# A two-layer hybrid attention block in fp32r on one core: compression tiles first in the head, a finer step of the compressed softmax, GpSimd work in smaller pieces, kept down chunks, and head banks from the ending layer's pool

## The chip, the cores and the metric

The kernel runs on one core of one Trainium2 chip. The time is device microseconds of one execution of the whole program, both layers, from the inputs in device memory to the output there. Weights are read from device memory in every execution. Lower is better.

## What is computed

For 512 tokens of width 1024 two layers are applied, each with a mixer and a feed-forward part:

```python
def hybrid_mixer(h, ...):
    q_nsa, kv_nsa, g_nsa, qkv_sb, g_merge = split(h @ w_in)
    q, k_cmp, k_slc, k_win = rope(...)          # v_cmp, v_slc, v_win as they are
    kc = gelu(blocks_of_32(k_cmp, stride 16) + pe @ w1 + b1) @ w2    # 31 compressed keys; vc alike
    o_nsa = g0 * softmax(q kc) vc + g1 * selected_attention(...) + g2 * window_attention(...)
    o_sb = stick_breaking_attention(...)        # 8 heads
    return (sigmoid(ga) * (o_nsa @ w_proj_nsa) + sigmoid(gb) * (o_sb @ w_proj_sb)) @ w_out
for l in range(2):
    x = x + rms_norm(hybrid_mixer(rms_norm(x)))
    h = rms_norm(x)
    x = x + rms_norm((gelu(conv3(h @ w_up)[gate]) * conv3(h @ w_up)[up]) @ w_down)
```

There are 8 query heads in 2 groups of 4, head width 64, and 2816 hidden units. With 8 selection blocks of 64 tokens and up to 16 selected, the selection takes all blocks, so that selected and window attention are both causal attention.

## The kernel before, in words

**Splits.** Every product is made of three matmuls in fp32r, hi x hi, lo x hi and hi x lo, where a value is the sum of a rounded part (hi) and the rest (lo). `h_hi` and `h_lo` hold the layer's input, normed, as [128, 8, 512]. Weights come through the class `Weights` (L54): a raw chunk of 128x1024 (512 KB) is fetched by SP's queue into one of three buffers, ScalarE (ACT) rounds it into `whi` (L105), and `wlo` is the difference (L106), made by VectorE (DVE), or by GpSimd (POOL) for 13 weights of a layer that are used beside the attention. `whi` and `wlo` have two buffers each. `gemm` and `mm` (L381 to L387) issue the matmuls; a `drain` runs one tile's to its end.

**Order of the work.** The kernel is written in Tile: the program says what reads and writes what, buffers and their counts say what may be in flight, and a scheduler fixes the order of each engine when the kernel is built, with `tc.high_priority()` as a hint. Instructions of an engine run in that fixed order, so one that waits holds up all that stand behind it. PSUM has a pool "pg" with six banks "bk" (closed before the attention), and helper banks with one buffer each, among them "f", which serves all the fill tiles of the attention: a fill tile can begin only when DVE has emptied the one before.

**Head of a layer.** The first six tiles of `w_m` in the order of `_cols` (L1284: the two key tiles kv(2) and kv(4), q tiles 0 and 1, then kv(0) and kv(1), the inputs of the compression) are computed in two halves of the tokens, the first half in `head_first` (L496) while the chain of the norm for the second half still runs, the second in `head_second` (L512). Each finished tile is handled by the loop at L667. `rope` (L610) copies the bank to `rf` on ACT, sends four `rs` transfers of 32 partitions through SP (L619), multiplies by cosine (`rt`) and sine (`rs`) and hands the two to a function that adds them: `k_tile` (L638) writes the split `kst` and sends two transfers, `q_tile` (L632) writes the split `qst`, `kc_done` (L662) writes `kd` and calls `spread` (L656), which sends `cstk` in four transfers. The second part of a rope is put off by one tile (`flush_later(1)`). The last tile, the compression's v, needs no rope.

Then come the value tiles `acc4` (L682), four banks of 128x280 with the values `vN` (hi on ACT at L704, lo on DVE at L706) and the gates' logits (L708, ACT); then `cst`, the split of `cstk` (L710 to L713), q tiles 2 and 3 (L715), and 32 compression matmuls into two more banks `cps` (L722). As there are six banks in all, the two of `cps` are those of the first two value tiles. The hidden layer of the compression follows (L735 to L746).

**Attention.** A pipeline over 32 subs, each one head of one block of 128 queries (`Sub`, loop at L978): scores `S`, maximum, exponential, scale of P by GpSimd (L924), transposes, and per pair of heads a product `pv`. `cmp_scores` (L846) is a generator with three stops that makes the softmax over the compressed keys for one group of heads (L854 to L870) and is stepped by the same loop, twice in each of two turns; `cmp_transpose` (L872) follows in the next turn:

```python
d = n - 15 * g_
if d == 2: cg = cmp_scores(g_)
if 2 <= d < 4:
    next(cg)
    next(cg, None)
if d == 4: pcs[g_] = cmp_transpose(g_)
```

Between the subs' matmuls the scheduler puts the fill tiles of the stick-breaking heads and of the merge: `sb_pair` (L772, emptied by `sbz` L781 and split at L786 to L789), `gate` (L795, emptied at L802), `sb_values` (L809). The stick-breaking attention, the output projections and the feed-forward part with its convolution follow.

**End of a layer.** The down projection has eight tiles of 22 row blocks in chunks of 8, 8 and 6. The last three (`TAIL_D`, m = 5, 6, 7) are computed for each half of the tokens apart (`down_tile`, L1250), so that the norm of the first half (`chain`, L426) runs beside the second half's; their weights are fetched and split twice. The pool with these banks is closed at the end of the layer, and the next head's six banks come from a new one, used in the order 1 to 5, 0.

Of the kernel before, what the change touches and what calls it, by code (L numbers as in the profile page):

```python
# [33 lines left out]
TAIL_D = 3  # L34

# [18 lines left out]
class Weights:  # L54
# [27 lines left out]
    def split(self, upto):  # L82
        while self.n_split <= min(len(self.items) - 1, upto):
# [4 lines left out]
            if fold:  # L88
# [8 lines left out]
                continue  # L97
            if dest is None:
# [5 lines left out]
            for c in ((slice(0, n),) if i else (slice(0, n // 2), slice(n // 2, n))):  # L104
                self.nc.scalar.copy(hi[:, c], raw[:, c])  # L105
                eng.tensor_sub(lo[:, c], raw[:, c], hi.bitcast(F)[:, c])  # L106
# [4 lines left out]
    def get(self):  # L111
        i = self.n_got
        self.n_got += 1
        self.ensure(i)
        return self.parts.pop(i)

# [42 lines left out]
def run_kernel(ctx, tc, xT, pos, inv, vec, pew, cw1, w_m, w_vn, w_pr, w_o, w_u, w_d, xmid, rot, out):  # L159
# [25 lines left out]
    for l in range(DEPTH):  # L185
# [19 lines left out]
        for i in dts:  # L205
            k0 = 0
            for n in DCH:
                it(w_d[l, i, :, k0 * 128:(k0 + n) * 128], n * 128)
# [315 lines left out]
    for l in range(DEPTH):  # L524
# [33 lines left out]
        pg = pg_ctx.enter_context(pool("pg", space=PSUM))  # L558
# [4 lines left out]

        banks = [bank() for _ in range(HEAD)]
        banks = banks[1:] + banks[:1]
# [15 lines left out]
        with temps(6) as ip:  # L581
# [85 lines left out]
            for i in head_second(banks, kept, n_pre=HEAD):  # L667
                b = banks[i]
                if i < 2:
                    k_tile(i, b)  # L670
                elif i < 4:
                    q_tile(i - 2, b)
                elif i == 4:
                    rope(b, kc_done)
                else:
# [3 lines left out]
                flush_later(1)  # L679

# [4 lines left out]
            for n_kt in (3, 3, 2):  # L685
# [11 lines left out]
                flush_later()  # L697
                kt += n_kt
# [10 lines left out]

            for v in range(2):  # L710
                src = cstk[:, v].rearrange("p (m s) -> p s m", s=8)
                nc.scalar.copy(cst[:, v, 0, :, :66], src)
                nc.vector.tensor_sub(cst[:, v, 1, :, :66], src, cst.bitcast(F)[:, v, 0, :, :66])  # L713
# [21 lines left out]
            for v in range(2):  # L735
                part = ip.tile([64, 132], F, name=nm("cpart"), tag="cpart")
                sums = ip.tile([64, 66], F, name=nm("csum"), tag="csum")
                nc.scalar.copy(part, cps[v][64:128, :132])
                nc.vector.tensor_add(part, cps[v][:64, :132], part)
# [99 lines left out]
        with temps(0) as nt, pool("pn", space=PSUM) as pn:  # L839
# [43 lines left out]
            class Sub:  # L883
# [35 lines left out]
                def scale(self):  # L919
# [4 lines left out]
                    nc.gpsimd.tensor_mul(pv, pv, st[:, None, 2:4, None].to_broadcast([128, self.i + 1, 2, 128]))  # L924
# [50 lines left out]
            pcs, cps_ = {}, {}  # L975
            subs[0].scores()
            at_sub = lambda n: subs[n] if 0 <= n < N else None
            for n in range(N + 3):  # L978
# [238 lines left out]
        with temps(5) as ft_:  # L1217
# [32 lines left out]
            def down_tile(m, tr, side=None):  # L1250
# [3 lines left out]
                for n_ in DCH:  # L1254
# [103 lines left out]
```

## Time and profile before

| | |
|---|---|
| time, median of 3 runs | 1655.97 us (1655.7 to 1656.61) |
| the profiled execution: its own time | 1653.88 us |
| its span, first to last instruction | 1652.2 us |
| mean granted TensorE clock in it | 0.989 of 2.4 GHz |
| busy: TensorE (PE), its weight loads (PEld) | 1609.0 us (97%), 1393.2 us (84%) |
| busy: DVE, ACT, POOL | 1118.2 (68%), 825.3 (50%), 211.1 us (13%) |
| DMA | 159.42 MB, mean 96 GB/s |

The table is one execution. A matmul of 512 columns starts every 0.23 us at full clock; the profile gives each a longer duration, since they are pipelined, so gaps between starts tell more than busy shares. The lines that matter stand in the section of rows below: where PE waited and for whom, the clock that was granted in a stretch, and the timelines of the engines that it waited for.

### The profile page before, as it was taken

To read this page: it belongs to the slowest core of one execution; us is meant where nothing else is said; L and a number is where in the kernel's file an instruction comes from. 1 tells how busy PE (TensorE), PEld (TensorE's weight loads), DVE (VectorE), ACT (ScalarE), POOL (GpSimd) and SP (SyncE) were. 2 spreads that over 40 slices of the span, in tenths; PEclk is the share of its full clock that TensorE was granted. 3 is DMA by queue.
4 is the path that set the end of the run, shared out by engine and by line. 5 is a ranking of instruction groups with operands and counts; after the bars stand their busy time and mean duration, and the time that the engine had idled before them with its cause. 6 is when DMAs were issued, how large, how long until landed. Compare 5 with 4: busy or idle time off the path is not lost.

```text
span 1652.2 us, 23212 instructions
## 1 busy us (share of the span) xinstructions
PE 1609.0 (97%) x8970; PEld 1393.2 (84%) x8970; DVE 1118.2 (68%) x1659; ACT 825.3 (50%) x1338; POOL 211.1 (13%) x252
## 2 busy tenths in 40 slices
PE   9899999999999999999999999999999999999997
PEld 9878887888998888888998788878889988888896
DVE  8775676767578777733677666677676687776235
ACT  6555565654555444423555455575536454444233
POOL 0034442120000000000000453322200000000000
PEclk9989999999999999999999999999999999999999
DMA  6521112114412233333664211112153132322344
GB/s 228 152 77 52 39 39 64 52 64 141 132 61 88 91 102 91 97 93 107 195 204 129 71 44 47 39 64 64 52 180 114 39 99 93 102 91 95 98 128 141
DMA packets 53501, 159.42 MB, mean 96 GB/s; under 512 B 6544, under 2 KB 12176, under 8 KB 53392
## 3 DMA queue, kind: packets, MB, share of 16 engines
q1 hardware_dynamic: 51088, 152.00, 29.0%
q0 software_dynamic: 1296, 4.72, 0.8%
q8 instruction: 70, 1.15, 0.3%
q10 hardware_dynamic: 1008, 1.23, 0.3%
q14 instruction: 39, 0.32, 0.1%
HBM read 144.30 MB, written 4.72 MB: 90 GB/s over the span
## 4 chain that ended last, share of the span: by engine, by line
PE 82%; DVE 8%; ACT 5%; issue 2%; DMA 2%; POOL 1%; SPq 1%; ACTq 0%; DVEq 0%; POOLq 0%
PE bk L382 56%; PE f L382 15%; PE pv L382 3%; PE Z L382 3%; PE S L382 2%; PE tp L935 2%; POOL sbt L1034 1%; DVE wlo L106 1%; DVE st L906 1%; DMA rs<-rf 1%; DMA x<-in_xT 1%; ACT whi L105 0%; ACT sbt L226 0%; ACT sbt L1058 0%; ACT sbw L226 0%
## 5 line engine op out<-in xcount | busy, mean ns | idle before, releaser
L105 ACT CAST whi<-wraw 128x1024 fp32r<-128x1024 f32 (+2 forms) x235 | 241.2, 1027 | 342.7 <-PE bk L382 254.3
L106 DVE TENSOR_TENSOR wlo<-wraw,whi 128x1024 fp32r<-128x1024 f32 (+2 forms) x209 | 248.8, 1191 | 184.1 <-ACT whi L105 181.4
L382 PE MATMUL bk<-h_hi,whi 128*128 128x512 f32 (+1 forms) x768 | 286.5, 374 | 2.1 <-ACT f_t L1260 1.7
L382 PE MATMUL bk<-h_hi,wlo 128*128 128x512 f32 (+1 forms) x768 | 286.4, 374 | 0.0
L382 PE MATMUL bk<-h_lo,whi 128*128 128x512 f32 (+1 forms) x768 | 286.2, 373 | 0.0
L382 PE MATMUL f<-h_hi,whi 128*128 128x512 f32 x448 | 184.4, 412 | 11.7 <-DVE gate L802 9.2
L382 PE MATMUL f<-h_lo,whi 128*128 128x512 f32 x448 | 179.1, 400 | 0.0
L382 PE MATMUL f<-h_hi,wlo 128*128 128x512 f32 x448 | 178.6, 399 | 0.0
L382 PEld LDWEIGHTS bk<-h_hi,whi 128*128 128x128 f32 x768 | 145.6, 190 | 27.7 <-ACT f_t L1260 1.9
L382 PEld LDWEIGHTS bk<-h_hi,wlo 128*128 128x128 f32 x768 | 145.5, 190 | 25.4 <-DVE wlo L106 0.4
L382 PEld LDWEIGHTS bk<-h_lo,whi 128*128 128x128 f32 x768 | 145.6, 190 | 24.8
L382 PE MATMUL bk<-ah,wlo 128*128 128x256 f32 (+1 forms) x484 | 161.7, 334 | 2.4 <-DVE wlo L106 2.4
L382 PE MATMUL bk<-ah,whi 128*128 128x256 f32 (+1 forms) x484 | 160.4, 331 | 0.0
L382 PE MATMUL bk<-al,whi 128*128 128x256 f32 (+1 forms) x484 | 160.2, 331 | 0.0
L382 PEld LDWEIGHTS f<-h_hi,whi 128*128 128x128 f32 x448 | 86.4, 193 | 30.6 <-DVE gate L802 10.0
L382 PEld LDWEIGHTS bk<-ah,wlo 128*128 128x128 f32 x484 | 91.8, 190 | 12.5 <-DVE wlo L106 3.4
L1228 DVE TENSOR_TENSOR cu<-bk,r 128x512 f32<-128x512 f32 x88 | 60.2, 687 | 61.2 <-PE bk L382 60.9
L382 PEld LDWEIGHTS f<-h_hi,wlo 128*128 128x128 f32 x448 | 85.9, 192 | 18.5
L382 PEld LDWEIGHTS f<-h_lo,whi 128*128 128x128 f32 x448 | 86.5, 193 | 15.5
L382 PEld LDWEIGHTS bk<-ah,whi 128*128 128x128 f32 x484 | 91.9, 190 | 8.7
L382 PEld LDWEIGHTS bk<-al,whi 128*128 128x128 f32 x484 | 91.9, 190 | 8.7
L382 PE MATMUL bk<-h_hi,wh 128*128 128x256 f32 x512 | 96.0, 285 | 0.0
(241 smaller groups left out, 3174.3 us busy)
## 6 DMA issues: line engine op xcount, KB each, us to landing
wraw<-in_w_u SPq DMA_DIRECT2D x88, 512.0 KB, 3.5
wraw<-in_w_m SPq DMA_DIRECT2D x72, 512.0 KB, 3.3
wraw<-in_w_d SPq DMA_DIRECT2D x44, 512.0 KB, 3.5
wraw<-in_w_d SPq DMA_DIRECT2D x22, 384.0 KB, 3.1
wraw<-in_w_pr SPq DMA_DIRECT2D x16, 512.0 KB, 3.6
wraw<-in_w_o SPq DMA_DIRECT2D x16, 512.0 KB, 3.5
rs<-rf SPq DMA_DIRECT2D x56, 64.0 KB, 2.8
wraw<-in_cw SPq DMA_DIRECT2D x4, 512.0 KB, 4.6
```

The costliest lines, as they stand in the source:

```text
L105: self.nc.scalar.copy(hi[:, c], raw[:, c])
L106: eng.tensor_sub(lo[:, c], raw[:, c], hi.bitcast(F)[:, c])
L382: last_mm[0] = nc.tensor.matmul(o, a, b, start=first, stop=last, skip_group_check=True)
L906: nc.vector.tensor_reduce(self.st[:, 0:2], self.S[:, :self.n].rearrange("p (j b k) -> p b j k", j=self.i + 1, b=2), axis=AX.XY, op=OP.max, ...
L935: nc.tensor.transpose(tp[:, b * 128:(b + 1) * 128], self.P[:, (c + b) * 128:(c + b + 1) * 128], ident)
L1034: nc.gpsimd.affine_select(out=d, in_=d, compare_op=OP.is_gt, fill=0.0, base=0, pattern=[[1, 128]], channel_multiplier=-1)
L1228: nc.vector.tensor_mul(u, b, r2)
```

## The change

There are five parts. (1) The tiles of the compression, k and v, come first in `_cols`, then the two key tiles and q tiles 0 and 1; the head loop follows, and the `cst` splits move into the loop of the value tiles, behind its first chunk. (2) The softmax of the compressed scores is stepped once per turn (turns 2 to 5), its transposes come in turn 6, the second group starts two turns earlier, and a `pv` product that needs it waits in a list until it is there. (3) GpSimd makes `wlo` in four pieces of 256 columns, and scales P in pieces of 256 columns. (4) The first two chunks of down tile 6 are split into the second token half of `h_hi` and `h_lo`, which is free then, and serve both halves, so that they are not fetched again. (5) The six banks of layer 1's head are taken from the pool of the ending layer, one by one as they come free and in their own order; that pool is closed behind the head, and a new one serves the value tiles, q tiles 2 and 3 and the compression.

```diff
@@ Weights.split @@
+            if isinstance(dest, tuple):
+                hi, lo = dest
+                raw = raw.rearrange("p (s c) -> p s c", c=256)
+                self.nc.scalar.copy(hi.whole(), raw)
+                eng.tensor_sub(lo.whole(), raw, hi.whole().bitcast(F))
...
-                eng.tensor_sub(lo[:, c], raw[:, c], hi.bitcast(F)[:, c])
+                step = (c.stop - c.start) // (4 if eng is self.nc.gpsimd else 1)
+                for c_ in range(c.start, c.stop, step):
+                    s = slice(c_, c_ + step)
+                    eng.tensor_sub(lo[:, s], raw[:, s], hi.bitcast(F)[:, s])
@@ class Strips @@
+    def whole(self):
+        return self.t()[:, self.k:self.k + 4, 256:]
...
@@ items @@
+                keep = i == KEPT and c < 2
+                if not (keep and j >= 8):
+                    it(w_d[l, i, :, k0 * 128:(k0 + n) * 128], n * 128,
+                       dest=(Strips(lambda: h_hi, 4 * c), Strips(lambda: h_lo, 4 * c)) if keep else None)
@@ banks of the head @@
-        banks = [bank() for _ in range(HEAD)]
-        banks = banks[1:] + banks[:1]
+        if l == 0:
+            pf_ctx = ExitStack()
+            pg = pf_ctx.enter_context(pool("pg", space=PSUM))
+            next_banks = [bank() for _ in range(HEAD)]
+        banks = next_banks
@@ head loop @@
-                if i < 2:
-                    k_tile(i, b)
-                elif i < 4:
-                    q_tile(i - 2, b)
-                elif i == 4:
+                if i == 0:
                     rope(b, kc_done)
+                elif i >= 4:
+                    q_tile(i - 4, b)
+                elif i >= 2:
+                    k_tile(i - 2, b)
                 else:
...
+            pf_ctx.close()
+            pg = pg_ctx.enter_context(pool("pg", space=PSUM))
@@ after the first chunk of the value tiles (before: behind them) @@
+                if kt == 0:
+                    for v in range(2):
+                        src = cstk[:, v].rearrange("p (m s) -> p s m", s=8)
+                        nc.scalar.copy(cst[:, v, 0, :, :66], src)
+                        nc.vector.tensor_sub(cst[:, v, 1, :, :66], src, cst.bitcast(F)[:, v, 0, :, :66])
@@ hidden layer of the compression @@
-                part = ip.tile([64, 132], F, name=nm("cpart"), tag="cpart")
+                part = ip.tile([64, 132], F, name=nm("cpart"), tag="cpart", bufs=2)
...
+                with tc.high_priority():
+                    nc.scalar.copy(part, cps[v][64:128, :132])
+                    nc.vector.tensor_add(part, cps[v][:64, :132], part)
@@ Sub.scale @@
-                    nc.gpsimd.tensor_mul(pv, pv, st[:, None, 2:4, None].to_broadcast([128, self.i + 1, 2, 128]))
+                    for j in range(self.i + 1):
+                        nc.gpsimd.tensor_mul(pv[:, j], pv[:, j], st[:, 2:4, None].to_broadcast([128, 2, 128]))
@@ loop over the subs @@
-                    d = n - 15 * g_
+                    d = n - 13 * g_
                     if d == 2:
                         cg = cmp_scores(g_)
-                    if 2 <= d < 4:
-                        next(cg)
+                    if 2 <= d < 6:
                         next(cg, None)
-                    if d == 4:
+                    if d == 6:
                         pcs[g_] = cmp_transpose(g_)
                 if s3 and s3.hm == 1:
-                    pv_pair(s3)
+                    pv_due.append(s3)
+                while pv_due and pv_due[0].g in pcs:
+                    pv_pair(pv_due.pop(0))
@@ down_tile @@
-                for n_ in DCH:
-                    drain(gemm(b[:, :w_], W.get(), *a_of(tr), range(k0, k0 + n_), first=k0 == 0,
+                for c, n_ in enumerate(DCH):
+                    keep = m == KEPT and c < 2
+                    wt = kept_d[c] if keep and tr is HALVES[1] else W.get()
+                    if keep:
+                        kept_d[c] = wt
+                    drain(gemm(b[:, :w_], wt, *a_of(tr), range(k0, k0 + n_), first=k0 == 0,
@@ end of a layer @@
             if last:
                 side_next.finish()
-        pf_ctx.close()
+                pf_ctx.close()
+            else:
+                next_banks = [bank() for _ in range(HEAD)]
@@ _cols @@
-    tiles = [kv(2), kv(4), q(0), q(1), kv(0), kv(1), q(2), q(3)]
+    tiles = [kv(0), kv(1), kv(2), kv(4), q(0), q(1), q(2), q(3)]
```

The change moves instructions on every engine. Three places, as the orders have them; lines of the changed kernel are some 30 to 40 higher.

Place 1, PE of layer 0, from the end of the last q tile (`bk_899` before, `bk_903` now) over the compression matmuls into two banks to a fill tile (`f`). Before (the first fill tile, `f_2182`, has 24 matmuls, of which the last three are shown):

```order
L382 MATMUL f_2182<-h_hi,whi_951 128x512
L382 MATMUL f_2182<-h_lo,whi_951 128x512
L382 MATMUL f_2182<-h_hi,wlo_952 128x512
L382 MATMUL bk_933<-cst_473,wh_63_722 128x132 x16
L382 MATMUL bk_934<-cst_473,wh_69_839 128x132 x16
L382 MATMUL f_2227<-h_hi,whi_2207 128x512
L382 MATMUL f_2227<-h_lo,whi_2207 128x512
```

Now:

```order
L413 MATMUL bk_903<-h_hi,whi_665 128x512
L413 MATMUL bk_903<-h_lo,whi_665 128x512
L413 MATMUL bk_903<-h_hi,wlo_666 128x512
L413 MATMUL bk_937<-cst_473,wh_60_712 128x132 x16
L413 MATMUL bk_938<-cst_473,wh_70_847 128x132 x16
L413 MATMUL f_2234<-h_hi,whi_955 128x512
L413 MATMUL f_2234<-h_lo,whi_955 128x512
L413 MATMUL f_2234<-h_hi,wlo_956 128x512
L413 MATMUL f_2234<-h_hi,whi_955 128x512
```

In before `bk_899` ends just ahead of `f_2182`, and the compression follows that fill tile; now it follows the q tile, and the first fill tile stands behind it.

Place 2, DVE of layer 0, the readers of the value banks (`vN`) and the ropes of q tiles 0 and 1 (`qst_4_104`, from `rt` and `rs`). Before:

```order
L706 SCALAR_TENSOR_TENSOR vN_732<-bk_733,rT_465,vN_732 128x2x64 x2
L630 TENSOR_TENSOR rt_593<-rt_593,rs_592 128x512
L706 SCALAR_TENSOR_TENSOR vN_732<-bk_734,rT_465,vN_732 128x2x64 x2
L706 SCALAR_TENSOR_TENSOR vN_732<-bk_735,rT_465,vN_732 128x2x64 x2
L706 SCALAR_TENSOR_TENSOR vN_732<-bk_736,rT_465,vN_732 128x2x64 x2
L623 TENSOR_TENSOR rs_639<-rs_639,cs_t_462 128x512
L620 TENSOR_TENSOR rt_685<-rf_683,cs_t_462 128x512
L636 SCALAR_TENSOR_TENSOR qst_4_104<-rt_593,qst_4_104 64x512 x2
L630 TENSOR_TENSOR rt_640<-rt_640,rs_639 128x512
L623 TENSOR_TENSOR rs_684<-rs_684,cs_t_462 128x512
L106 TENSOR_TENSOR wlo_952<-wraw_681,whi_951 128x1024
L664 TENSOR_TENSOR kd_477<-rt_685,rs_684 128x256x2
```

Now:

```order
L652 TENSOR_TENSOR rt_719<-rf_717,cs_t_462 128x512
L655 TENSOR_TENSOR rs_672<-rs_672,cs_t_462 128x512
L662 TENSOR_TENSOR rt_673<-rt_673,rs_672 128x512
L668 SCALAR_TENSOR_TENSOR qst_4_104<-rt_673,qst_4_104 64x512 x2
L655 TENSOR_TENSOR rs_718<-rs_718,cs_t_462 128x512
L662 TENSOR_TENSOR rt_719<-rt_719,rs_718 128x512
L668 SCALAR_TENSOR_TENSOR qst_4_104<-rt_719,qst_4_104 64x512 x2
L746 SCALAR_TENSOR_TENSOR vN_736<-bk_737,rT_465,vN_736 128x2x64 x2
L746 SCALAR_TENSOR_TENSOR vN_736<-bk_738,rT_465,vN_736 128x2x64 x2
L746 SCALAR_TENSOR_TENSOR vN_736<-bk_739,rT_465,vN_736 128x2x64 x2
L746 SCALAR_TENSOR_TENSOR vN_736<-bk_740,rT_465,vN_736 128x2x64 x2
```

The four `vN` pairs stood ahead of both `qst` (the second follows two rows below the ones shown) and now stand behind both; on ACT the gates of each value bank follow its `vN`, so they are moved too.

Place 3, DVE of layer 0, the end of the first softmax over the compressed keys (`cp`, `cm`) and the operation that empties the bank "f". Before:

```order
L860 TENSOR_TENSOR cp_1093<-cp_1093,cm_1096 128x512
L922 TENSOR_TENSOR st_1127<-st_1127,gates_111 128x2
L863 TENSOR_REDUCE cm_1096<-cp_1093 128x16
L864 RECIPROCAL cm_1096<-cm_1096 128x16
L867 TENSOR_TENSOR cm_1096<-cm_1096,gates_111 128x16
L802 TENSOR_TENSOR gate_2342<-f_2343,r_90 128x512
```

Now:

```order
L896 TENSOR_TENSOR cp_1097<-cp_1097,cm_1117 128x512
L958 TENSOR_TENSOR st_1126<-st_1126,gates_111 128x2
L899 TENSOR_REDUCE cm_1117<-cp_1097 128x16
L900 RECIPROCAL cm_1117<-cm_1117 128x16
L817 SCALAR_TENSOR_TENSOR sbz_2397<-f_2363,r_90 128x512
L903 TENSOR_TENSOR cm_1117<-cm_1117,gates_111 128x16
```

The operation that empties "f" (`gate_2342` before, `sbz_2397` now) stood behind the product of `cm` with the gates and now stands ahead of it.

## Rows read from the trace of the kernel before

**Rows 1.** The page: busy time, the chain's shares by engine, the DMA issues of the ropes.

```profile
PE 1609.0 (97%) x8970; PEld 1393.2 (84%) x8970; DVE 1118.2 (68%) x1659; ACT 825.3 (50%) x1338; POOL 211.1 (13%) x252
...
PE 82%; DVE 8%; ACT 5%; issue 2%; DMA 2%; POOL 1%; SPq 1%; ACTq 0%; DVEq 0%; POOLq 0%
...
rs<-rf SPq DMA_DIRECT2D x56, 64.0 KB, 2.8
```

**Rows 2.** Waits of PE by releaser: total us, times, longest.

```profile
PE f L382 <- DVE gate L802: 9.2, 4, 4.0
PE bk L382 <- DVE cst L713: 3.4, 2, 1.9
PE bk L382 <- DVE wlo L106: 2.4, 3, 1.4
...
PE bk L382 <- ACT f_t L1260: 1.7, 1, 1.7
```

**Rows 3.** Windows: length, busy us of each engine, granted clock, DMA share, GB/s.

```profile
76.00:88.00 12.00, 10.12 (x47) 9.05 (x46) 10.44 (x14) 6.11 (x9) 0.34 (x1) 0.72 0.46 134
99.00:126.00 27.00, 22.99 (x109) 18.58 (x109) 20.64 (x38) 11.38 (x32) 11.51 (x8) 0.87 0.22 70
190.00:260.00 70.00, 66.42 (x409) 55.54 (x408) 46.95 (x100) 37.16 (x95) 25.72 (x16) 1.00 0.11 39
814.00:832.00 18.00, 14.32 (x115) 13.69 (x113) 15.16 (x24) 12.62 (x21) 1.48 (x2) 1.00 0.76 249
```

**Rows 4.** Timeline of PE, compression of layer 0, and at 908: start us, us, instruction.

```profile
72.34 0.39 PE L382 MATMUL f<-h_hi,whi 128*128 128x512 f32 x1
...
77.55 0.39 PE L382 MATMUL f<-h_hi,wlo 128*128 128x512 f32 x1
79.82 1.43 PE L382 MATMUL bk<-cst,wh 128*128 128x132 f32 x10 [1.88 <-DVE cst L713]
...
85.75 0.73 PE L382 MATMUL f<-h_hi,whi 128*128 128x512 f32 x1
...
93.12 0.50 PE L382 MATMUL f<-h_hi,whi 128*128 128x512 f32 x1
...
908.27 0.50 PE L382 MATMUL f<-h_hi,whi 128*128 128x512 f32 x1
```

**Rows 5.** Timeline of SP's DMA issues, layer 0.

```profile
65.44 3.19 SPq L619 DMA_DIRECT2D rs<-rf  x4
...
73.44 2.42 SPq L660 DMA_DIRECT2D cstk<-kd  x4
```

**Rows 6.** Timeline of DVE, ropes and values of layer 0.

```profile
64.50 0.61 DVE L706 SCALAR_TENSOR_TENSOR vN<-bk,rT,vN 128x128 fp32r<-128x128 f32 x2
...
68.50 1.41 DVE L636 SCALAR_TENSOR_TENSOR qst<-rt,qst 64x512 fp32r<-64x512 f32 x2
...
70.55 0.69 DVE L623 TENSOR_TENSOR rs<-rs,cs_t 128x512 f32<-128x512 f32 x1
...
83.46 0.69 DVE L623 TENSOR_TENSOR rs<-rs,cs_t 128x512 f32<-128x512 f32 x1 [1.07 <-DMA rs<-rf]
```

**Rows 7.** Timeline of PE, first softmax of the compressed scores.

```profile
120.19 0.80 PE L382 MATMUL f<-h_hi,whi 128*128 128x512 f32 x1 [4.01 <-DVE gate L802]
```

**Rows 8.** Timeline of DVE, same place.

```profile
117.19 2.34 DVE L867 TENSOR_TENSOR cm<-cm,gates 128x16 f32<-128x16 f32 x1
119.45 0.68 DVE L802 TENSOR_TENSOR gate<-f,r 128x512 f32<-128x512 f32 x1
120.05 0.16 DVE L868 TENSOR_TENSOR cm<-cm,rowv 128x16 f32<-128x16 f32 x1
```

**Rows 9.** Timeline of GpSimd (POOL), ahead of and at the same place.

```profile
98.29 0.61 POOL L924 TENSOR_TENSOR P<-P,st 128x256 f32<-128x256 f32 x1 [1.83 <-ACT P L226]
...
117.16 2.34 POOL L106 TENSOR_TENSOR wlo<-wraw,whi 128x1024 fp32r<-128x1024 f32 x1 [0.40 <-ACT whi L105]
```

**Rows 10.** Timeline of PE, first head tile of layer 1.

```profile
828.29 0.39 PE L382 MATMUL bk<-h_hi,whi 128*128 128x256 f32 x1 [1.67 <-ACT f_t L1260]
```

More of the change, by code (lines that the diff above doesn't have):

```diff
@@ L34 @@
 TAIL_D = 3
+KEPT = 6
 ALL = slice(0, T)
@@ L97, in split @@
                 continue
+            if isinstance(dest, tuple):
[3 more added lines that the diff above has]
+                eng.tensor_sub(lo.whole(), raw, hi.whole().bitcast(F))
+                self.parts[i] = dest
+                self.n_split += 1
+                self.prefetch()
+                continue
             if dest is None:
@@ L115, in get, with __init__, __getitem__ @@
         return self.parts.pop(i)
+class Strips:
+    def __init__(self, t, k):
+        self.t = t
+        self.k = k
+    def whole(self):
+        return self.t()[:, self.k:self.k + 4, 256:]
+    def __getitem__(self, key):
+        c, e = key[1].start, key[1].stop
+        return self.t()[:, self.k + c // 256, 256 + c % 256:256 + c % 256 + e - c]
 class Fill:
@@ L204, in run_kernel @@
         dts = list(range(8 - TAIL_D)) + 2 * list(range(8 - TAIL_D, 8))
-        for i in dts:
+        for j, i in enumerate(dts):
             k0 = 0
-            for n in DCH:
-                it(w_d[l, i, :, k0 * 128:(k0 + n) * 128], n * 128)
+            for c, n in enumerate(DCH):
+                keep = i == KEPT and c < 2
+                if not (keep and j >= 8):
+                    it(w_d[l, i, :, k0 * 128:(k0 + n) * 128], n * 128,
+                       dest=(Strips(lambda: h_hi, 4 * c), Strips(lambda: h_lo, 4 * c)) if keep else None)
                 k0 += n
@@ L557, in run_kernel @@
         pg_ctx = ExitStack()
-        pg = pg_ctx.enter_context(pool("pg", space=PSUM))
         def bank():
             return pg.tile([128, T], F, name=nm("bk"), tag="bk", bufs=6)
-        banks = [bank() for _ in range(HEAD)]
-        banks = banks[1:] + banks[:1]
+        if l == 0:
[3 more added lines that the diff above has]
+        banks = next_banks
         with temps(0) as hp:
@@ L708, in run_kernel @@
                 nc.scalar.activation(gates[:, j], acc4[j][:, 256:280], AF.Copy, scale=rj)
[L710 to L713, printed above, removed]
             qst.append(slot("q1", "qst1", FR))
@@ L735, in run_kernel @@
             for v in range(2):
-                part = ip.tile([64, 132], F, name=nm("cpart"), tag="cpart")
+                part = ip.tile([64, 132], F, name=nm("cpart"), tag="cpart", bufs=2)
                 sums = ip.tile([64, 66], F, name=nm("csum"), tag="csum")
-                nc.scalar.copy(part, cps[v][64:128, :132])
-                nc.vector.tensor_add(part, cps[v][:64, :132], part)
+                with tc.high_priority():
+                    nc.scalar.copy(part, cps[v][64:128, :132])
+                    nc.vector.tensor_add(part, cps[v][:64, :132], part)
                 nc.vector.tensor_add(sums, part[:, :66], part[:, 66:])
@@ L975, in run_kernel @@
             pcs, cps_ = {}, {}
+            pv_due = []
             subs[0].scores()
@@ L1260, in down_tile @@
                 nc.scalar.activation(f_t[:, m, tr], b[:, :w_], AF.Copy, scale=g_post2[:, m:m + 1])
+            kept_d = {}
             last = l == DEPTH - 1
```

## Prediction

> **What bounds the kernel now.** I read the page first. TensorE (PE) is busy for 1609.0 us, 97% of the span, and the chain that ended last lies on PE for 82% [rows 1]. No part of the change removes a matmul that counts, so all it can win is PE's idle time and the stretches in which PE runs at the lower of its two clock levels. Next, the waits of PE grouped by what ended them [rows 2]: two long ones in the fill tiles "f" behind a VectorE (DVE) `gate` (4 waits, 9.2 us, the longest 4.0), two before the compression matmuls behind `cst` (3.4), three behind `wlo` of the down tiles (2.4), one behind `f_t` at the layer boundary (1.7). Each of the first two comes once per layer. Then the windows [rows 3]: around the compression matmuls (76 to 88 us) the granted clock is 0.72, around the softmax of the compressed scores (99 to 126) it is 0.87. A stretch whose mean is 0.72 holds 56% of its time at half speed: 0.56 x 12 = 6.7 us at 1.2 instead of 2.4 GHz, which costs 3.4 us; 0.87 over 27 us gives 7.0 us and 3.5. So each of these waits is paid twice: as idle time, and as a slow stretch right behind it. The `cst` wait costs about 1.9 + 3.4 = 5.3 us, the `gate` wait 4.0 + 3.5 = 7.5 us, per layer.
>
> **The change, part by part, in its order on PE.**
>
> *Compression tiles first.* In before PE reaches the end of the q tiles at 72.34, does one fill tile (24 matmuls, 72.34 to 77.55), waits until 79.82 for `cst`, does the 32 compression matmuls (until 85.75, slow), then the second fill tile, and begins the third at 93.12 [rows 4]. The change makes `cst` ready early (its cast now stands on ACT and DVE ahead of the last key tile's), but the scheduler drew two conclusions from it that cost something. The compression matmuls now come right behind the q tiles, with no fill tile ahead (place 1 of the order). And they write into the banks of the first two value tiles; these are free only when DVE and ACT have read them (`vN`, `gates`), and in the changed order these readers stand behind the ropes of both q tiles (place 2). The last of the six head tiles is now q1, whose rope needs a transfer through SP. SP issues four `rs` transfers in 3.19 us and four `cstk` in 2.42 [rows 5]; the rope of q1 now has eight `cstk` issues ahead of it instead of two. I reckon its last issue at about 71.3 (the fourth rope's four issues ended at 65.44 + 3.19 = 68.6 in before; six `cstk` more are 3.6 us, the tail of one `kst` pair less), its landing 2.8 us later [rows 1] at 74.1, then on DVE the product `rs` 0.69, a sum of the same size, `qst` 1.41, `vN` 0.61 [rows 6], and ACT's small `gates`: free at 77.5 to 78. PE arrives at 72.9 (the start of the head loses about 0.5: its first value tile waits for an ACT copy behind a weight cast). So a wait of about 5 us stands where one of 1.9 stood, followed by the slow stretch as before.
>
> That puts the first fill tile at about 77.9 + 5.9 = 83.8 instead of the second one at 85.75. Its end, about 90.2, is followed by a further wait: there is one bank for "f", it is emptied by DVE's `sbz`, and this now stands behind the ropes of q tiles 2 and 3 (in before the last of their `rs` was there at 83.46 [rows 6]; here the queue is later by the same 5 us, so about 88, and a product, two sums, the `cpart` sums and two `qst` pairs follow): about 93.2. So at 93.2 the change begins its second fill tile where before began its third: one fill tile behind. A tile is 24 matmuls in 77.55 + 0.23 - 72.34 = 5.4 us. **Loss 5.5 us in layer 0.** Fill tiles are not free work, they are all needed later, so this stays lost. In layer 1 the same order stands, and before begins its third fill tile at 908.27 [rows 4]; I reckon the second of the change at 907.2 by the same steps, one tile less 1.1: **loss 4.4**. Ends per layer: nothing, if SP runs ahead of my count so that only what `cst` cost before is left (or a gain of the 5.3 if even this goes), and 8, if the later `sbz` slips by one more rope.
>
> *Softmax one step per head, GpSimd in pieces.* In before a fill tile of PE waits 4.01 us, until 120.19 [rows 7]. The reason is on DVE: `gate`, which empties the one "f" bank, starts at 119.45, behind a 128x16 product (L867) that took 2.34 us, when its neighbour of the same size (L868) took 0.16 [rows 8]. GpSimd ran its `wlo` from 117.16 for 2.34 us [rows 9]: the two end together. With `wlo` in four pieces of 256 columns the block is bounded by one piece, which I take from the 128x256 scaling, 0.61 [rows 9]. The changed order also has the evacuation of "f" right behind the reciprocal and ahead of that product (place 3), so even that block no longer stands before it. The product started at 117.19, behind the reciprocal; an evacuation in its place takes 0.68, so PE resumes at 117.9 in the place of 120.19, and earlier by as much as DVE is ahead from not being blocked at the two earlier `wlo`s. That is 2.3 us of idle time; whether the slow stretch goes as well depends on what is left of the wait. Idle gaps of about 2 us were followed by half speed at 77.55 and not at the layer boundary (1.67) [rows 3, 4, 10], so what is left, 1.7 or less, is on the better side. Ends: 2.3 (clock still falls) and 7.5 (no wait at all). I take 5.4, near 2.3 + 3.5: **gain 5.4 per layer**.
>
> The Trainium skill ("SBUF — State Buffer", Who interferes with whom) says that a VectorE operation with two SBUF inputs and a GpSimd operation that reads SBUF exclude each other for a whole instruction, and that whichever starts first wins. The trace agrees with the first half (2.34 beside 2.34). By the second half the pieces also open gaps in which DVE can hold GpSimd up; that is the rival C below.
>
> *The other stalls of attention.* In 190 to 260 us PE is busy for 66.42 of 70 [rows 3]: some 3.6 us in gaps under 1.4 us. One step of softmax per head and smaller blocks take some of it away; the deferred output products and the scaling in pieces (0.61 for each 256 columns, more instructions on an engine that is busy 13%) put something new there. Bounds -2 and +3 per layer; I take **+1 per layer**, near the middle.
>
> *Kept down chunks, head banks.* Two weight chunks less per layer are 2 DMAs, 2 ACT casts, 2 DVE subtractions. PE doesn't get shorter; what counts is the wait behind `wlo` (2.4 in all) and the first head tile's wait for its bank behind `f_t` (1.7) [rows 2, 10]. With banks from the ending pool in turn the first head tile takes a bank that has long been free: gain 1.7. The `wlo` of the last tile's second chunk still stands behind the post chain on DVE, so I count little there: **2.0 in all**, ends 0 and 4. At the end of the kernel the same chunks may take **0.5** (0 to 1).
>
> **Sum**, against the profiled execution (1653.88): -5.5 + 5.4 - 4.4 + 5.4 + 2 x 1 + 2.0 + 0.5 = 5.4 us less, 1648.5. The median of the runs shown is 2.1 us above that execution, so about 1650.6: I say **1651**, 0.3% faster.
>
> **Rivals.** A change within 0.2% (3.3 us) is about what can't be told from none.
>
> A, slower. The new wait before the compression matmuls decides: it keeps its 5.5 and 4.4 (the order shows the readers behind the ropes), while at the softmax the clock still falls, so the gain there is 2.3 twice, and attention wins nothing: -9.9 + 4.6 + 2.5 = 2.8 worse; with 1 us lost per layer in attention, 5 worse: about 1661. It decides from the point at which the softmax gives less than about 3.7 a layer. For it: a residual wait of about 1.7 lies just under one that was followed by half speed. Chance 0.23.
>
> B, much faster. q1's transfers are issued in time, since SP waits less for DVE than I count, and the compression matmuls no longer wait. Then 5.3 and 7.5 per layer go, and the 2.5: 28 us, about 1628. Against it: SP's issues are a plain sum of durations of which none shrinks. Chance 0.07.
>
> C, no change. Terms cancel, within 3.3 us: about 1655. One way: GpSimd's pieces are held up by DVE operations of 0.69 each, 4 x 0.69 = 2.8 us more per `wlo`, and PE waits for that once per layer: 5.6 of the gain go. The rule of the page named above is that rival. Against it: GpSimd is idle most of the time between its `wlo`s. Chance 0.05 for this way, 0.20 for other cancelling.
>
> **How the numbers follow.** The forecast (3.3 to 15 us faster) has 0.45, B 0.07: faster 0.52; C, same 0.25; A, slower 0.23. The range reaches from 1641 (softmax waits gone wholly, 4 more, attention and boundary at their better ends, 6 more) to 1661 (A); B and the worst of A lie outside.
>
> **What would show it.** In the changed profile: the first compression matmul at 77 to 79 us, with a wait of 4 to 6 before it that ends with ACT `gates` or DVE `vN`, and a second fill tile that starts at about 93 and waits for `sbz`; no DVE operation of 128x16 over 0.9 us; the fill-tile wait near 116 under 2 us and the clock of that stretch 1.00; no wait for `f_t` at the boundary. The prediction is wrong if the compression matmuls start by 74, or if a wait of over 3 us stands in the fill tiles after 95 us.

## The result, and the profile after

The changed kernel takes 1667.76 us (median of 4 runs, 1667.15 to 1668.28) against 1655.84 of the kernel before: 1.0073 times, 95% interval 1.0055 to 1.0090. It is 12 us slower, outside the range that was forecast.

The page after, busy time of the engines, answers to [rows 1]:

```profile
PE 1605.1 (96%) x8970; PEld 1393.1 (84%) x8970; DVE 1097.0 (66%) x1655; ACT 820.5 (49%) x1334; POOL 239.1 (14%) x426
```

TensorE (PE) works as long as before; the span grew from 1652.2 to 1666.2 us. The time went into waits, so the waits of PE come first (total us, times, longest), against [rows 2]:

```profile
PE bk L413 <- ACT rf L648: 22.5, 3, 15.8
PE f L413 <- DVE sbz L817: 10.6, 3, 6.4
...
PE bk L413 <- ACT gates L748: 1.0, 1, 1.0
...
PE f L413 <- DVE gate L838: 0.9, 1, 0.9
```

The waits for `gate` fell from 9.2 to 0.9, and those for `cst` and `f_t` are gone. In their place stand 22.5 us in which a bank "bk" waits for ACT to copy a rope's tile out (`rf`), 15.8 of them in one piece, and 10.6 us for `sbz`. The windows (length, busy us of PE, PEld, DVE, ACT, POOL, granted clock, DMA share, GB/s), the first four those of [rows 3], the last one the place of the long wait:

```profile
76.00:88.00 12.00, 10.97 (x53) 9.36 (x52) 5.93 (x13) 6.96 (x15) 0.34 (x1) 0.76 0.25 77
99.00:126.00 27.00, 26.54 (x132) 21.82 (x133) 20.40 (x47) 18.48 (x48) 12.83 (x17) 0.93 0.26 79
190.00:260.00 70.00, 69.36 (x432) 58.69 (x430) 42.33 (x92) 39.72 (x97) 32.91 (x54) 1.00 0.14 54
814.00:832.00 18.00, 17.47 (x144) 17.14 (x143) 17.23 (x30) 11.91 (x23) 1.48 (x2) 1.00 0.60 194
866.00:890.00 24.00, 8.17 (x51) 7.96 (x51) 16.04 (x23) 8.11 (x12) 0.82 (x2) 0.64 0.61 169
```

The stages come some 7 us later than before, so a window doesn't hold quite the same work; still, three are better: PE is busy for 26.54 of 27 us around the compressed softmax (22.99 before), 69.36 of 70 in the attention (66.42), 17.47 of 18 at the layer boundary (14.32). With the windows moved by 7 us the three values are 27.00 at a clock of 1.00, 67.93 and 17.47, so the attention gained less than the row suggests. Two stretches are new and bad: from 866 to 890 PE is busy for 8.17 of 24 us, at a mean clock of 0.64, and from 84 to 104, just ahead of the softmax, for 13.58 of 20 at 0.71 (19.94 at 0.91 before).

By the start of the first matmul of each stage in PE's timeline, before and after: value tiles of layer 0 48.47 and 49.23, first down tile 700.58 and 707.98, value tiles of layer 1 864.42 and 883.70, last matmul 1641.47 and 1655.18. So layer 0 lost 7.4, the way from its down tiles to layer 1's value tiles 11.9 more, and the rest won 5.6 back.

The long wait in layer 1, in the timeline of PE (start us, us, instruction, idle time before it and what ended it):

```profile
867.59 0.28 PE L413 MATMUL bk<-h_hi,wh 128*128 128x256 f32 x1
883.70 0.83 PE L413 MATMUL bk<-wh,h_hi 128*128 128x280 f32 x2 [15.83 <-ACT rf L648]
```

And the timeline of ACT there:

```profile
865.61 1.06 ACT L648 COPY rf<-bk 128x512 f32<-128x512 f32 x2
...
872.69 0.58 ACT L648 COPY rf<-bk 128x512 f32<-128x512 f32 x1 [3.75 <-DMA rs<-rf]
876.50 1.14 ACT L736 CAST cst<-cstk 128x528 fp32r<-128x528 f32 x1 [3.22 <-DMA cstk<-kd]
880.13 1.26 ACT L682 CAST kst<-rt 64x512 fp32r<-64x512 f32 x2 [2.49 <-DVE rt L675]
881.41 0.59 ACT L648 COPY rf<-bk 128x512 f32<-128x512 f32 x1
882.02 1.14 ACT L736 CAST cst<-cstk 128x528 fp32r<-128x528 f32 x1
883.06 0.58 ACT L648 COPY rf<-bk 128x512 f32<-128x512 f32 x1
```

The first value tile starts at 883.70, right behind the last of the five ropes' copies (883.06 + 0.58), that of q1. The copies come late for two reasons, which the rows show. The third (872.69) waits for the `rs` transfers of an earlier rope, since each rope takes some of a few work buffers (a median of 2.3 us from issue to landing in this run, 2.8 in [rows 1]). The last two stand in ACT's fixed order behind the casts of `cst` and `kst`, which wait for `cstk` and for DVE's `rt`, and so for transfers too. In the built program the six head tiles of layer 1 stand in PSUM banks 7, 6, 5, 4, 3 and 2 in their order, and the value tiles in 2, 7, 6 and 5: the first one on the bank of q1.

In layer 0 the same kind of wait comes in smaller pieces, again in PE's timeline:

```profile
49.23 0.52 PE L413 MATMUL bk<-wh,h_hi 128*128 128x280 f32 x2 [2.82 <-ACT rf L648]
...
56.85 0.53 PE L413 MATMUL bk<-wh,h_hi 128*128 128x280 f32 x2 [3.86 <-ACT rf L648]
```

Then comes what was forecast for the compression, on PE and, below, on DVE:

```profile
79.53 4.75 PE L413 MATMUL bk<-cst,wh 128*128 128x132 f32 x32 [1.03 <-ACT gates L748]
...
99.46 0.79 PE L413 MATMUL f<-h_hi,whi 128*128 128x512 f32 x1 [6.42 <-DVE sbz L817]
```

```profile
77.16 1.39 DVE L668 SCALAR_TENSOR_TENSOR qst<-rt,qst 64x512 fp32r<-64x512 f32 x2 [0.70 <-ACT qst L667]
78.56 1.12 DVE L746 SCALAR_TENSOR_TENSOR vN<-bk,rT,vN 128x128 fp32r<-128x128 f32 x4
...
88.76 0.69 DVE L655 TENSOR_TENSOR rs<-rs,cs_t 128x512 f32<-128x512 f32 x1 [4.63 <-DMA rs<-rf]
89.37 1.22 DVE L119 TENSOR_TENSOR wlo<-wraw,whi 128x1024 fp32r<-128x1024 f32 x1
...
95.03 0.69 DVE L655 TENSOR_TENSOR rs<-rs,cs_t 128x512 f32<-128x512 f32 x1 [0.96 <-DMA rs<-rf]
...
97.14 1.40 DVE L668 SCALAR_TENSOR_TENSOR qst<-rt,qst 64x512 fp32r<-64x512 f32 x2 [0.62 <-ACT qst L667]
...
98.72 0.68 DVE L817 SCALAR_TENSOR_TENSOR sbz<-f,r 128x512 f32<-128x512 f32 x1
```

`vN` stands on DVE behind the last `qst` (77.16) and runs at 78.56; ACT's `gates` release the compression matmuls at 79.53, forecast for 77.5 to 78. But PE waits only 1.0 us for them, not the 5 of the forecast: it ends the q tiles at 78.5 in place of 72.9, since the value tiles had waited for `rf` and a stretch at the lower clock had followed (0.44 us for a matmul that takes 0.29 at full clock). The second fill tile starts at 99.46, forecast for 93.2: the last `rs` product waits at 95.03, since SP issued these transfers only at 91.00, behind a weight fetch issued at 90.62, when the `wlo` of 89.37 had freed its buffer at 90.59. The forecast had not laid that fetch into SP's queue.

At the softmax of the compressed keys, the timeline of DVE against [rows 8] and, below it, of GpSimd against [rows 9]:

```profile
123.35 0.63 DVE L817 SCALAR_TENSOR_TENSOR sbz<-f,r 128x512 f32<-128x512 f32 x1
123.90 0.17 DVE L903 TENSOR_TENSOR cm<-cm,gates 128x16 f32<-128x16 f32 x1
```

```profile
107.65 3.73 POOL L119 TENSOR_TENSOR wlo<-wraw,whi 128x256 fp32r<-128x256 f32 x4 [1.24 <-ACT whi L115]
...
115.22 3.71 POOL L119 TENSOR_TENSOR wlo<-wraw,whi 128x256 fp32r<-128x256 f32 x4 [2.70 <-ACT whi L115]
```

The 128x16 product takes 0.17 us, where it took 2.34, and the evacuation of the fill bank stands ahead of it. GpSimd's four pieces take 3.73 us together, where one `wlo` took 2.34 to 2.40. These are the longest; 20 of the 26 sets of four in this trace take 2.8. In the long ones a piece takes up to 1.20 us where it runs beside a DVE operation with two inputs, and 0.73 else. No wait of PE names them.

### The profile page after: what moved, and what is told of

It reads as the page before. It is cut to its first block, busy times and chain, and to the rows that moved or that the text cites. A ratio compares the mean times of both kernels' runs of the same rounds, so it can differ in the third digit from the quotient of the medians.

```text
span 1666.2 us, 23416 instructions
## 1 busy us (share of the span) xinstructions
PE 1605.1 (96%) x8970; PEld 1393.1 (84%) x8970; DVE 1097.0 (66%) x1655; ACT 820.5 (49%) x1334; POOL 239.1 (14%) x426
## 5 line engine op out<-in xcount | busy, mean ns | idle before, releaser
L115 ACT CAST whi<-wraw 128x1024 fp32r<-128x1024 f32 (+2 forms) x227 | 233.0, 1027 | 341.8 <-PE bk L413 260.6
L119 DVE TENSOR_TENSOR wlo<-wraw,whi 128x1024 fp32r<-128x1024 f32 (+2 forms) x201 | 238.9, 1190 | 199.2 <-ACT whi L115 197.2
L413 PE MATMUL f<-h_hi,whi 128*128 128x512 f32 x448 | 182.9, 408 | 15.1 <-DVE sbz L817 10.6
L413 PEld LDWEIGHTS bk<-h_hi,whi 128*128 128x128 f32 x768 | 145.0, 189 | 27.5 <-ACT whi L115 1.2
L413 PE MATMUL bk<-ah,wlo 128*128 128x512 f32 (+1 forms) x420 | 142.6, 340 | 0.5 <-DVE wlo L119 0.5
L413 PE MATMUL bk<-ah,whi 128*128 128x512 f32 (+1 forms) x420 | 142.3, 339 | 0.0
L413 PE MATMUL bk<-al,whi 128*128 128x512 f32 (+1 forms) x420 | 142.2, 338 | 0.0
L961 POOL TENSOR_TENSOR P<-P,st 128x256 f32<-128x256 f32 x160 | 94.1, 617 | 111.9 <-DVE st L958 79.6
L413 PEld LDWEIGHTS f<-h_lo,whi 128*128 128x128 f32 x448 | 86.2, 192 | 15.3
L983 DVE TENSOR_TENSOR pt<-tp,pt 128x512 fp32r<-128x512 f32 (+1 forms) x96 | 56.6, 594 | 55.1 <-ACT pt L981 45.9
L413 PEld LDWEIGHTS bk<-ah,wlo 128*128 128x128 f32 x420 | 79.6, 190 | 9.4 <-DVE wlo L119 0.7
```

Of the source, the lines that this page charges most:

```text
L119: eng.tensor_sub(lo[:, s], raw[:, s], hi.bitcast(F)[:, s])
L413: last_mm[0] = nc.tensor.matmul(o, a, b, start=first, stop=last, skip_group_check=True)
L961: nc.gpsimd.tensor_mul(pv[:, j], pv[:, j], st[:, 2:4, None].to_broadcast([128, 2, 128]))
L983: nc.vector.tensor_sub(lo[:, :w_, self.hm], src, hi.bitcast(F)[:, :w_, self.hm])
```

## The experiments

"The ring" is the changed kernel without the closing of the head's pool. Each run stood beside runs of the kernel before on the same chip; the times are medians, the ratios with their intervals are those to the kernel before.

### Is it the pool?

**The ring.** The pool stays open until the compression is done:

```diff
...
-            pf_ctx.close()
-            pg = pg_ctx.enter_context(pool("pg", space=PSUM))
+            if l:
+                pg = pf
...
-        pg_ctx.close()
+        pf_ctx.close()
```

> The changed kernel, but the pool of the head's six banks is not closed behind the head: value tiles, q tiles 2 and 3 and the compression take their banks from the same ring, so that the first value tile takes the bank of the first head tile. Theory (the new pool puts layer 1's first value tile on the bank of the last rope, q1): the 16 us wait of the value tiles in layer 1 falls to what layer 0 shows (3 to 4 us twice), the slow stretch behind it shortens; 1651 to 1656 us. Rival (the tile order makes the ropes late, whatever bank): the wait keeps over 10 us and the time stays above 1662.

1640.23 us, ratio 0.9892 (0.9876 to 0.9908): 27.5 us faster than the changed kernel and 1.1% faster than the one before. Its waits:

```profile
PE f L413 <- DVE sbz L816: 8.3, 3, 3.8
...
PE S L413 <- DVE cpart L774: 3.3, 2, 2.0
...
PE bk L413 <- ACT gates L747: 0.3, 1, 0.3
```

No wait for `rf` is left. The theory holds and was too cautious, because the closing had cost in layer 0 as well: there the compression matmuls now start right behind the q tile, with no gap, on PE:

```profile
73.67 0.40 PE L413 MATMUL bk<-h_hi,wlo 128*128 128x512 f32 x1
73.90 3.69 PE L413 MATMUL bk<-cst,wh 128*128 128x132 f32 x32
```

In the ring `vN` runs from 62.8 us on, ahead of both `qst`. So the order of `vN` behind the ropes, on which the recorded loss rested, does not belong to the tile order but to the pool; the two closed kernels in the old tile order, further on, have it as well. In the built program the value tiles of layer 1 stand in banks 6, 7, 5, 4: an open pool gave them the banks that are read first.

**A pool of its own per layer** (part 5 undone wholly: the hunks "banks of the head", `pf_ctx.close()` behind the head, and "end of a layer").

> The changed kernel without its part 5: each layer's head opens a pool of its own, with the banks rotated by one as before. Theory (bank places): no wait of over 5 us before the value tiles of layer 1; the wait for f_t at the layer boundary (1.7 us) comes back; 1653 to 1658 us. Rival (tile order): over 10 us stay, above 1662.

1642.05, ratio 0.9906 (0.9891 to 0.9921). The wait for `f_t` (1.7) is back, the 16 us are gone; as in the ring, the time is better than the theory gave.

**Part 5 alone** on the kernel before:

> The kernel before with part 5 alone (head banks of layer 1 from the ending pool, pool closed behind the head). Theory (the harm is that the new pool's first bank is that of the head's last tile, which in the changed tile order has a rope and in the old one has none): no wait over 5 us before the value tiles of layer 1, the wait for f_t (1.7) gone, 1652 to 1656 against 1656 of before. Rival (closing a pool makes the next one wait for all of its readers): a wait of 8 or more there, the time above 1661.

1670.18, ratio 1.0079 (1.0064 to 1.0094): 13 us slower, and this theory fell. Of the rival the time came out, but not the wait of 8 us or more; the value tiles wait in turn, and the compression and the fill tiles behind them:

```profile
PE f L382 <- DVE sbz L785: 11.0, 4, 4.5
PE bk L382 <- ACT rf L617: 10.1, 4, 3.1
PE bk L382 <- ACT gates L712: 4.7, 1, 4.7
```

So the bank of the last tile is not the whole harm. The next two runs part the closing from the handover.

**Closing alone** (kernel before, own pool per layer; between the head loop and the value tiles):

```diff
+            pg_ctx.close()
+            pg_ctx = ExitStack()
+            pg = pg_ctx.enter_context(pool("pg", space=PSUM))
```

> The kernel before, with its head pool closed behind the head and a new one opened for the value tiles, in both layers; no banks from the ending layer. Theory (a fresh pool fixes the value tiles to the banks of the head in turn, where an open one gives them the bank that is released first; they then wait for ropes one by one, and vN slips behind the ropes): nearly all of the 13 us that part 5 alone cost, 1666 to 1672. Rival (the handover from the ending layer costs): 1654 to 1659.

1669.33, ratio 1.0073 (1.0050 to 1.0095). On PE in layer 0:

```profile
49.31 0.52 PE L382 MATMUL bk<-wh,h_hi 128*128 128x280 f32 x2 [2.82 <-ACT rf L616]
...
55.89 0.83 PE L382 MATMUL bk<-wh,h_hi 128*128 128x280 f32 x2 [3.25 <-ACT rf L616]
...
60.66 0.84 PE L382 MATMUL bk<-wh,h_hi 128*128 128x280 f32 x2 [2.29 <-ACT rf L616]
```

Three value tiles wait one after the other for the copies of three head tiles. The fresh pool's banks come in the head's order, whatever is read first. On DVE `vN` runs at 79.8 here, behind the first two `qst` pairs. The 12.8 us by which this run is slower are net of something that it wins. Where the kernel before waits 4.0 us for `gate` in each layer (9.2 in all, [rows 2]), a wait of 1.64 for `sbz` stands here; the sum of the waits for `gate`, and the place in layer 0:

```profile
PE f L382 <- DVE gate L806: 1.2, 2, 0.6
```

```profile
125.53 0.50 PE L382 MATMUL f<-h_hi,whi 128*128 128x512 f32 x1 [1.64 <-DVE sbz L785]
```

**Handover alone** (kernel before, with layer 1's banks from the ending pool, kept open as in the ring):

> The kernel before, with layer 1's head banks taken from the ending layer's pool, which stays open until the compression is done. Theory (the closing costs, the handover saves the wait for f_t and what lies behind): 1652 to 1656. Rival: 1660 or more.

1656.14, ratio 0.9995 (0.9984 to 1.0007): no change. The wait for `f_t` is gone; in layer 1 the wait for `cst` rose from 1.6 to 3.1 us in its place.

**Closing without the handover** in the changed kernel, so that the first value tile gets the bank of the head's first tile in both layers:

> The changed kernel without the handover of banks, but with the pool closed behind the head in both layers. Theory (which bank comes first decides): layer 1 shows what layer 0 shows, waits of 3 and 4 us for rope copies in place of 16, and the time lies 3 to 8 us under the changed kernel's 1667.8: 1660 to 1665. Rival (any fresh pool waits for the last rope): the 16 us stay, 1667 or more with the f_t wait back.

1664.61, ratio 1.0044 (1.0029 to 1.0059), in the theory's range.

```profile
PE f L413 <- DVE sbz L817: 10.9, 2, 5.6
PE bk L413 <- ACT gates L748: 5.9, 2, 4.9
PE bk L413 <- ACT rf L647: 5.2, 3, 2.8
```

The 16 us are gone with the bank: the longest wait for `rf` is 2.8, in layer 0, and in layer 1 it is 0.2, less than the 3 to 4 that were expected. But only 3 us of time come back (5 by the two ratios), since in layer 1 the compression now waits 4.9 us for `gates` and a fill tile 5.3 for `sbz`, which stand behind the same ropes. Most of the loss is thus the delay of the whole chain value tiles, `vN`, compression, `sbz`; the long wait is its most visible form.

### What the other parts are worth

**Pieces alone** (part 3 on the kernel before):

> The kernel before with part 3 alone (GpSimd in pieces of 256 columns). Theory: the 128x16 product falls from 2.34 to under 0.9 us and the wait at the compressed softmax from 4.0 to about 2.3 us or less per layer; if the clock then stays up, 6 to 10 us faster than before (1646 to 1650), else 3 (1653). Rival (pieces are held up by DVE themselves, and the order moves): no gain, 1655 to 1659.

1643.62, ratio 0.9917 (0.9901 to 0.9932): 13 us.

**`wlo` in pieces, the scaling of P whole:**

```diff
-                eng.tensor_sub(lo[:, c], raw[:, c], hi.bitcast(F)[:, c])
+                step = (c.stop - c.start) // (4 if eng is self.nc.gpsimd else 1)
...
```

> The kernel before with GpSimd's wlo in four pieces, the scaling of P as before. Theory (the 2.34 us block came from a whole wlo): most of the 13 us that both pieces gave, 1642 to 1647. Rival (the scaling of 512 to 1024 columns blocks as well): 1648 to 1653.

1643.03, ratio 0.9918 (0.9892 to 0.9945): all of it comes from `wlo`. On DVE, at the place of [rows 8], and the window of [rows 3]:

```profile
117.20 0.18 DVE L870 TENSOR_TENSOR cm<-cm,gates 128x16 f32<-128x16 f32 x1
117.30 0.69 DVE L805 TENSOR_TENSOR gate<-f,r 128x512 f32<-128x512 f32 x1
```

```profile
99.00:126.00 27.00, 27.00 (x142) 22.07 (x141) 18.83 (x45) 14.43 (x42) 16.29 (x20) 1.00 0.29 88
```

With the order of DVE as it was, the product takes 0.18, `gate` starts at 117.30 in the place of 119.45, PE is busy throughout, and the clock stays at 1.00 (0.87 before): both halves of the price are won back. By the medians that is 13.5 us, 6.7 per layer; between the two profiled executions, of which the one before lies 2.6 us under its median, it is 10.8, 4.8 of it in layer 0 up to its down tiles and 6.0 in layer 1 from its value tiles on.

**Pieces and steps** (parts 2 and 3):

> The kernel before with parts 2 and 3 (softmax one step per turn, pieces). Theory: both waits at the softmax nearly gone, 1643 to 1649. Rival (with the steps spread out, something else of the attention waits, as the 6.4 us wait for sbz in the changed kernel shows): 1653 to 1660.

1641.20, ratio 0.9898 (0.9881 to 0.9914). The steps add 2.4 us to what the pieces gave, about as much as the spread of these runs.

**The ring with the scaling of P whole:**

> The ring with the scaling of P in one operation per sub, as before. If the scaling never blocked DVE for long, the same as the ring, 1639 to 1642; if blocks of 1 to 2 us come back, 1643 to 1648.

1645.13, ratio 0.9924 (0.9907 to 0.9940): 4.9 us slower than the ring, with intervals that just touch (0.9876 to 0.9908 for the ring). The small scalings seem to count here, where on the kernel before they did not; which of the ring's other parts makes the difference was not tried.

**Tile order alone** (part 1):

> The kernel before with part 1 alone (compression tiles first). Recorded prediction: it loses a fill tile per layer, 5.5 and 4.4, so about 1665. Rival, after the run with the ring: the order costs nothing by itself, since the scheduler then places vN early, 1653 to 1659.

1655.61, ratio 0.9996 (0.9987 to 1.0005): no change, so the tile order by itself does not lose the recorded 9.9 us. It is a balance of waits: those for `cst` (3.4) are gone and those for `gate` fell from 9.2 to 1.2, while those for `sbz` rose from 1.6 to 13.9.

**Kept chunks alone** (part 4):

> The kernel before with part 4 alone (kept down chunks). Recorded prediction: the waits for wlo at the end of layer 0 (2.4) shrink by 0 to 2.4 and the end of the kernel by 0 to 1: 1653 to 1656. Rival: the split into h puts a new wait in the chain of the norm, 1657 to 1660.

1652.95, ratio 0.9975 (0.9964 to 0.9986): 4 us, at the upper end of the recorded bounds. At the end of layer 0 the wait of 1.39 for `wlo` is gone, and one of 0.54 stays where 0.62 stood. The way from the first down tile of layer 0 to layer 1's value tiles is 2.4 us shorter, and the way from layer 1's first down tile to the end 1.3.

**Parts 2, 3 and 4**, and the same with the handover in an open pool:

> The kernel before with parts 2, 3 and 4. If the tile order is worth nothing, as much as the changed kernel with its own pool per layer (1642); if it costs a fill tile per layer as recorded, 1632 to 1636; if it gains (the cst wait goes), 1644 to 1648. From the run with pieces and steps (1641) less the kept chunks' 0 to 3, I expect 1638 to 1641.

> All of the change but its tile order (part 1), and without the closing of the pool: parts 2, 3, 4 and the handover. If the terms add up from the run with parts 2, 3 and 4 (1640.3): less 1.7 to 4 for the f_t wait, 1636 to 1639. If the old tile order's wait for cst still costs more than the new order's waits, no better than the ring with the new order (1640).

1640.34 (ratio 0.9897, 0.9882 to 0.9912) and 1640.83 (0.9901, 0.9880 to 0.9923). Neither the handover nor the tile order adds anything that can be told apart; without the tile order a wait for `cst` of 3.6 us stands in layer 1.

**The ring with one more `wlo` on GpSimd:**

```diff
-            it(w_m[l, i], eng=nc.vector if i in (8, 9, 10) else nc.gpsimd)
+            it(w_m[l, i], eng=nc.vector if i in (8, 9) else nc.gpsimd)
```

> The ring with one more wlo per layer (weight tile 10) made by GpSimd in place of DVE. Theory (DVE holds up sbz behind the ropes, one wlo of 1.2 us less helps): 1637 to 1639. Rival (DVE's other waits fill the place, or GpSimd's 2.4 us are late): 1640 to 1642.

1642.65, ratio 0.9910 (0.9895 to 0.9924): no better; the waits for `sbz` stay at 8.0 us.

The fastest kernels are the ring, the change with a pool of its own per layer, and the three of this section with parts 2 and 3 in them and the old tile order: all lie between 1640 and 1642 and are not to be told from each other. The ring is 1.1% faster than the kernel before and 1.6% faster than the change as it was made (1640.23 to 1667.76).

## Why the prediction was wrong

**The step that failed** is "Kept down chunks, head banks ... 2.0 in all, ends 0 and 4". It costed the pool's handover and its closing at the gain of one wait, and never asked which bank the first value tile gets from the new pool, and what must be read out of it first. Closing costs 12.8 us by itself (1669.33 against 1656.51) and 27.5 in the changed kernel (1667.76 against 1640.23).

Of these 27.5 us the sum held 9.9, put down to the tile order; the other 17.6 are nearly all that it missed, since its gains, 15.3 without those 9.9, are near the 17 that the ring has. That the closing costs twice as much in the changed kernel is in part explained: some 3 us come with the handover (1664.61 to 1667.76), and on the kernel before the closing also does away with the two 4 us waits for `gate`, which in the changed kernel the pieces had removed already. Beside a closed pool parts 1 to 4 gain only 4.7 us (1669.33 to 1664.61), with a pool of its own per layer 15.6 (1657.67 to 1642.05). How much of that difference is the `gate` waits, and whether the tile order costs something once the pool is closed, no run separates.

Had the head's banks been followed through the new pool, the line `pf_ctx.close()` behind the head was the place to stop at: all six banks have readers there, five of them rope copies that wait for transfers.

**Compression tiles first, layer 0.** The chain was read rightly from the order: `vN` behind the ropes, `gates` at 77.5 to 78 (measured 79.5), then the wait for `sbz`. The first fill tile starts at 84.08, forecast for 83.8, but that is partly luck: the one wait of 5 us that was to lead there is 1.0, and the rest was lost earlier, at the value tiles. The cause was put on the wrong part. The order that was read was that of the whole change; the tile order alone (no change) and the ring (compression at 73.90 with no wait) show that it came from the closed pool. The size was also short: by its down tiles layer 0 lost 7.4 us, where the sum (-5.5 + 5.4 + 1) has a gain of 0.9. Two terms were missing, the 3.9 us wait of a value tile that ended at 56.85, and the weight fetch in SP's queue between the last ropes, which put `sbz` at 98.72. The wait that followed, 6.4 us until 99.46, is the sign that the prediction had named against itself: a wait of over 3 us in the fill tiles after 95 us.

**"In layer 1 the same order stands ... 4.4".** The order does stand there (`vN` runs at 896.7, behind both `qst`), but it is not what costs most: the first value tile waited 15.8 us ahead of it. The head's banks of layer 1 come from another pool than those of layer 0, which the prediction described and then didn't use.

**Softmax and pieces, 5.4 per layer.** Right in its mechanism and somewhat low: 6.7 per layer from `wlo` alone (13.5 in all), since the clock stayed up, near the upper end of 7.5. The step's main reason holds too: `gate` at 117.3 was reckoned for 117.2, though there by an evacuation ahead of the product, while in that run the product itself became short.

**Rival A** gave the sign, by a wait before the compression and a softmax that gains little. The sign came out, the mechanism did not: the waits for `gate` at the softmax are gone (9.2 to 0.9), and the clock there is 1.00 from 106 to 133 us. **Rival C's** way, GpSimd's pieces held up by DVE, does take place: four pieces took up to 3.73 us for 2.34 to 2.40 of one `wlo`. That agrees with the Trainium skill ("SBUF — State Buffer", Who interferes with whom): whoever starts first holds the shared ports for its whole instruction. Smaller instructions hand them over more often, and here a piece of 0.73 us takes up to 1.20 beside DVE. The waits of PE show none for these `wlo`, so its price was nothing.

**Other stalls of attention, +1 per layer; kept chunks.** The steps gave at most 2.4 in all, the kept chunks 4.0 where the sum had 2.0 for them and the `f_t` wait together. The `f_t` wait went as forecast and was worth nothing by itself (the handover alone: no change).

With the measured sizes the sum closes only for the ring: 13 for `wlo`, 2 for the steps, up to 4 for the kept chunks and 0 for tile order and handover make 15 to 19, and the ring is 17 faster than before in its own comparison (1657.67 to 1640.23). The closing then takes 27.5 of these away, 11.9 by the first down tile of layer 0 (696.13 in the ring, 707.98) and, between the profiled executions (27.2 in all), 15.3 in what follows.

What stays open is why the scheduler puts `vN` behind the ropes once the pool is closed. That it does is shown by the traces of the four kernels with a closed pool (the change, part 5 alone, closing alone, closing without the handover), in all of which both `qst` pairs come first; that it reckons with a later end of the value tiles is only argued.

## What to carry to other kernels

A pool that is closed and opened again is a set of waits: the new tiles get the banks in a fixed turn and each waits for the last reader of the old tile that lay there, while an open pool can give out the bank that is free first. Before costing such an edit at nothing, list for each of the next tiles the bank it gets and the last reader of that bank. And when several parts change an order together, build each part alone before a move in the order is put down to one of them.

## What the runs showed of the hardware

Cutting a GpSimd operation into four made it longer (2.8 us in most cases and up to 3.73, against 2.40) and the kernel faster, since DVE was no longer blocked for 2.3 us at a time: on the kernel before, this one line was worth 13 us. The idle time that it removed was two gaps of 4 us; the rest is the stretch at 1.2 GHz that had followed each (mean clock 0.87 in [rows 3], 1.00 after it). A change that lengthens every operation that it touches can thus pay, if another engine had waited for the whole of one.
